# First x rows on ScalarE's queue, second rows' squares, scalings and transposes in blocks 3 to 7, rotary tables behind the context rows

## The chip, the cores and the metric

The kernel runs on one core of a Trainium2 chip. The core has TensorE (PE in the profile; its weight loads are PEld), VectorE (DVE), ScalarE (ACT), GpSimd (POOL) and SyncE (SP), each with an instruction queue of its own, and 16 DMA engines that all of them share. The metric is the device time of one execution in microseconds (us); the median of several runs is compared.

## The reference

One layer of a diffusion backbone over 1024 latent tokens and 256 context tokens, 1024 wide. What matters here is its very beginning: the modulation vectors, the normalised and modulated rows, and the first of seven blocks of columns of the input projection (the values of the differential attention, 512 columns).

```python
def rms_norm(x, g):
    xf = x.astype(jnp.float32)
    y = xf * lax.rsqrt(jnp.mean(xf * xf, axis=-1, keepdims=True) + EPS)
    return (y * g.astype(jnp.float32)).astype(x.dtype)
...
        m_lat = sc @ w_mod[l] + b_mod[l]
        m_ctx = scc @ w_mod[l] + b_mod[l]
        sh1, sc1, g1, sh2, sc2, g2 = [t[:, None, :] for t in jnp.split(m_lat, N_MOD, axis=-1)]
        csh1, csc1, cg1, csh2, csc2, cg2 = jnp.split(m_ctx, N_MOD, axis=-1)

        h_lat = rms_norm(x, norm1_g[l]) * (1.0 + sc1) + sh1
        h_ctx = rms_norm(ctx, norm1_g[l]) * (1.0 + csc1) + csh1
        y_lat, y_ctx = token_mixers(h_lat, h_ctx, w_in[l], ret_decay_logit[l], ret_gn_g[l],
                                    diff_lambda[l], diff_subln_g[l], w_out[l], lambda_init,
                                    rope_r, rope_d, need_ctx=not last)
```

Everything is in float32. The rest of the layer (retention, differential attention, output projection, gated MLP with a convolution, final norm) follows and is the larger part of the time; the change does not touch it.

## The kernel before, in words

A float32 product is made of three passes over split operands (`passes`, L126 to L131): high by high, high by low, low by high. So every operand exists as a pair, `hT[0]`/`hT[1]` for the rows (`cT` for the context) and `whi`/`wlo` for weights.

The first stage (L490 to L710) computes, for each of the eight blocks k of 128 input columns:

- **the modulation** of that block: two loads of w_mod of 512 KB each (`mod_load`, tile `wt`, five buffers), eight products (`mod_part`), a copy (`mod_row`, tile `rw`), four small products (`mod_sums`, tile `pm`) and two evictions into `mcol`;
- **the rows**, turned: `latents(half, k)` transposes the block's columns of four row tiles on TensorE (L545, into a PSUM tile `pt`), and `modulate` makes the high part on ScalarE (L548), the float32 value `tmp` on VectorE (L550) and the low part `hT <- tmp,hT` (L552) on VectorE for even k and on POOL for odd k. `half` 0 is tokens 0 to 511 (row tiles 0 to 3, `xs0`), `half` 1 is tokens 512 to 1023 (row tiles 4 to 7, `xs1`). `tmp` has two buffers; `pt`, `pm` and a few others share three PSUM banks;
- **the products** of row tiles 0 to 3 with block k of the weights (`part_products`), six matmuls for each pair of tiles.

Before its columns can be turned, a row tile is loaded, squared and summed on ScalarE (`square`, L533), brought to its reciprocal root by a small operation on VectorE and a power on POOL (`power`, L114 and L115), and scaled on VectorE (`scale`, L539). Column 2 to 5 of `sm` belong to row tiles 0 to 3, column 6 to 9 to row tiles 4 to 7, 0 and 1 to the two context tiles.

Row tiles 4 to 7 are multiplied after the loop over k, 24 matmuls each, from the weights that are then all split: tiles 4 and 5 in this stage, with the function `between` putting other work between their blocks (the last latents, the stores `st` of tiles 0 to 3, the squares and scales of the context rows `xc`, and from tile 5 on the context's transposes), tiles 6 and 7 behind it. At the start and between the first modulations, `turn_over` issues matmuls on a tile of ones whose result is not used.

Two things set the order. Inside the stage, `in_order(begin)` chains all instructions of PE, DVE, ACT and SP from L594 on in the order in which the code stands; POOL is left out. Outside it, a scheduler places instructions by their dependencies, and may put one of a later stage between two of this one, as it does with the first split of the next stage's weights (`stream_block(5)`, L183 to L187). Loads all go through SP's queue, in order; a load takes one of eight completion semaphores in turn, so that the ninth load waits until the first has landed, and so on.

Of the kernel before, what the change touches and what calls it, by code (L numbers as in the profile page):

```python
# [17 lines left out]
P = 128  # L18
D = 1024
KD = D // P  # L20
# [52 lines left out]
def kernel(  # L73
# [16 lines left out]
    nc = tc.nc  # L90
    mm = nc.tensor.matmul
# [34 lines left out]
    def passes(ps, lt, rt, first, last, more=False):  # L126
        lh, ll = lt
        rh, rl = rt
        mm(ps, lh, rh, start=first, stop=False, skip_group_check=more)  # L129
        mm(ps, lh, rl, start=False, stop=False, skip_group_check=more)  # L130
        mm(ps, ll, rh, start=False, stop=last, skip_group_check=more)  # L131
# [20 lines left out]
    with ExitStack() as p1:  # L152
# [20 lines left out]
        hT = [[hp.tile([P, KD, 512], F32R, name=f"hT{a}{i}") for i in range(2)] for a in range(2)]  # L173
        xs0 = [xr.tile([P, D], F32, name=f"xs{t}") for t in range(4)]
        cT = []
        sm = hp.tile([P, 16], F32, name="sm")
# [320 lines left out]
        with ExitStack() as p0:  # L497
# [77 lines left out]
            def load_row(t):  # L575
                nc.sync.dma_start(out=xs0[t] if t < 4 else xs1[t - 4], in_=x[t * P : (t + 1) * P, :])

# [5 lines left out]

            def part_products(ts, k):
                for t in ts:
                    passes(part[t], lat_lhs(t, k), wget(k, 0, 512), k == 0, k == KD - 1)

# [6 lines left out]
            mod_load(0, 0)  # L594
            for t in range(3):
                load_row(t)
            mod_load(0, 1)
            load_row(3)
            w_load(0, 2)
# [4 lines left out]
            mod_part(0, 0)  # L604
            turn_over(10)
            square(xs0[0], 2)
# [13 lines left out]
            mod_sums(0)  # L620
            turn_over(4)
            scale(xs0[2], 4)
# [11 lines left out]
            for k in range(KD):  # L634
# [4 lines left out]
                if k < 2:  # L639
                    for q in range(2):  # L640
                        mod_part(k + 2, q)
                    mod_row(k + 2)
                if k == 7:
                    latents(1, 2)
                    latents(1, 3)
                if 1 < k < 6:
                    load_row(k + 2)
                n = k + 4
# [15 lines left out]
                if k == 3:  # L664
                    square(xs1[0], 6)
                    power(6)
                if k == 4:
                    square(xs1[1], 7)
                    scale(xs1[0], 6)
                    power(7)  # L670
                if k == 5:
                    first.close()
                    cp = pctx.enter_context(tc.tile_pool(name="cp", bufs=1, side="right"))
                    cT.extend(cp.tile([P, KD, LC], F32R, name=f"cT{a}") for a in range(2))
                    for t in range(NTC):
                        xc.append(xp.tile([P, D], F32, name="xc", tag="wt", bufs=5))
                        nc.sync.dma_start(out=xc[t], in_=ctxt[t * P : (t + 1) * P, :])
                    square(xs1[2], 8)
                    scale(xs1[1], 7)
                    power(8)  # L680
                    square(xs1[3], 9)
                    scale(xs1[2], 8)
                    power(9)
                    scale(xs1[3], 9)
                if k >= 6:
                    latents(1, 4 * (k - 6))
                    latents(1, 4 * (k - 6) + 1)
            for t in range(2):
                store(t, part[t])

            def between(t, k):
                if (t, k) == (4, 0):
                    latents(1, 6)
                    latents(1, 7)
                if (t, k) == (4, 1):
# [31 lines left out]
        pad(m2p, 128)  # L727
        rtab = load_rope(1)
        natural(wget, lat_lhs, range(6, NT), store)
# [804 lines left out]
```

## Time and profile before

| | us |
|---|---|
| median of 3 runs | 1408.58 (1408.39 to 1412.42) |
| the profiled execution | 1407.91 |
| its span, first to last instruction | 1406.1 |
| PE busy in the span | 1366.5 (97%) |
| DVE, ACT, POOL busy | 991.4, 729.6, 287.5 |
| PE busy in 0 to 10, 10 to 20 us | 5.09, 8.00 |
| PE busy in 20 to 50 us | 30.0 |
| PE busy in 50 to 60, 60 to 70 us | 7.01, 8.37 |
| DMA in 10 to 20, 50 to 60 us | 418, 24 GB/s |

How to read the profile: times are from the start of the span of one execution. A group is written as line, engine, operation, then output <- inputs by the names of the tiles, partitions x elements. The chain of waits is followed back from the last instruction of the span, at each step to what released it. Matmuls overlap each other, so the distance of two starts says more than the length of one.

### The profile page before, as it was taken

Reading aid. Unit: us, or ns where it says so; the run is one execution under the profiler, and the core shown is the slowest. Engines: PE = TensorE matmul, PEld = TensorE weight load, DVE = VectorE, ACT = ScalarE, POOL = GpSimd, SP = SyncE. Lnnn points to the kernel's source line nnn. Section 1 sums busy time; section 2 is a strip of 40 time slices with the busy share of each in tenths; the row PEclk is TensorE's granted clock in tenths of the full one; section 3 lists DMA queues with packets and bytes.
Section 4 is the critical chain, followed back from the end, with each engine's and each line's share of the span. In section 5 each row is a group of like instructions: output and inputs, shape, how many; then the busy total and the mean of one; then the engine's idle time right before and its main releaser. Section 6 shows DMA issues by size and latency. Waiting matters only on the chain.

```text
span 1406.1 us, 19426 instructions
## 1 busy us (share of the span) xinstructions
PE 1366.5 (97%) x7028; PEld 1147.6 (82%) x7028; DVE 991.4 (71%) x1445; ACT 729.6 (52%) x1391; POOL 287.5 (20%) x321
## 2 busy tenths in 40 slices
PE   8899999999999899999999999999999999999996
PEld 5688888888887799998888778888888888888885
DVE  3655874424686798886458987777787777897457
ACT  3553313333575689997136645555445555455533
POOL 1310000001656033411201242233332220000001
PEclk9999999999999999999999999999999999999999
DMA  9546885465575597622321223323323226953224
GB/s 336 224 151 200 284 278 188 134 182 172 177 242 159 175 208 170 126 66 85 141 98 45 97 98 113 113 90 113 105 105 113 96 79 219 397 175 104 91 97 179
DMA packets 96807, 218.81 MB, mean 156 GB/s; under 512 B 9220, under 2 KB 31236, under 8 KB 96200
## 3 DMA queue, kind: packets, MB, share of 16 engines
q1 hardware_dynamic: 88552, 192.67, 40.0%
q0 software_dynamic: 8160, 24.91, 7.8%
q8 instruction: 55, 0.90, 0.3%
q14 instruction: 40, 0.33, 0.1%
HBM read 160.13 MB, written 57.41 MB: 155 GB/s over the span
## 4 chain that ended last, share of the span: by engine, by line
PE 81%; issue 5%; DMA 5%; DVE 4%; ACT 2%; POOL 2%; SPq 0%; POOLq 0%; ACTq 0%; DVEq 0%
PE pv L869 5%; PE chain L129 5%; PE pA L837 5%; PE chain L131 5%; PE chain L130 5%; PE c L131 4%; PE c L129 4%; PE c L130 4%; PE pn L129 4%; PE pn L131 4%; PE pn L130 3%; PE pl L129 3%; PE pl L131 3%; PE pl L130 3%; PE third L129 2%
## 5 line engine op out<-in xcount | busy, mean ns | idle before, releaser
L129 PE MATMUL chain<-T,whi 128*128 128x512 f32 x264 | 103.5, 393 | 4.9 <-ACT ua L1250 3.9
L129 PE MATMUL pl<-hT,whi 128*128 128x512 f32 x256 | 106.2, 415 | 0.0
L130 PE MATMUL chain<-T,whi 128*128 128x512 f32 x264 | 103.5, 392 | 0.0
L131 PE MATMUL chain<-T,wlo 128*128 128x512 f32 x264 | 103.3, 392 | 0.0
L131 PE MATMUL pl<-hT,wlo 128*128 128x512 f32 x256 | 100.2, 391 | 0.0
L130 PE MATMUL pl<-hT,whi 128*128 128x512 f32 x256 | 100.0, 391 | 0.0
L840 DVE TENSOR_REDUCE mt<-pA 128x1 f32<-128x1280 f32 x64 | 95.3, 1490 | 3.6 <-PE pA L837 2.8
L837 PE MATMUL pA<-ks,qhl 128*128 128x512 f32 (+1 forms) x384 | 89.5, 369 | 2.7 <-ACT p L844 2.7
L131 PE MATMUL c<-whi,ghl 128*128 128x512 f32 x232 | 90.4, 390 | 0.0
L130 PE MATMUL c<-wlo,ghl 128*128 128x512 f32 x232 | 90.3, 389 | 0.0
L129 PE MATMUL c<-whi,ghl 128*128 128x512 f32 x232 | 90.3, 389 | 0.0
L844 ACT ACTIVATE p<-pA,mt 128x1280 f32<-128x1280 f32 x64 | 85.5, 1336 | 6.7 <-DVE mt L840 6.7
L1008 ACT CAST whi<-cmb 128x512 fp32r<-128x512 f32 x62 | 38.6, 623 | 86.7 <-PE chain L130 65.3
L837 PEld LDWEIGHTS pA<-ks,qhl 128*128 128x128 f32 x384 | 67.6, 189 | 14.8 <-ACT p L844 3.4
L129 PE MATMUL pn<-whi,hT 128*128 128x512 f32 x192 | 79.1, 412 | 0.0
L1163 POOL TENSOR_TENSOR cmb<-wrb 128x512 f32<-128x512 f32 x20 | 27.2, 1360 | 248.7 <-DMA wrb<-w_up 165.6
L869 PE MATMUL pv<-va,aT 128*128 128x128 f32 x640 | 77.0, 275 | 0.1
L131 PE MATMUL pn<-whi,hT 128*128 128x512 f32 x192 | 75.6, 394 | 0.9 <-POOL hT L552 0.4
L130 PE MATMUL pn<-wlo,hT 128*128 128x512 f32 x192 | 75.6, 394 | 0.0
L869 PEld LDWEIGHTS pv<-va,aT 128*128 128x128 f32 x640 | 74.0, 192 | 0.7 <-DVE yT L898 0.3
L1009 DVE TENSOR_TENSOR wlo<-cmb,whi 128x512 fp32r<-128x512 f32 x62 | 57.0, 922 | 23.0 <-ACT whi L1008 23.0
L115 POOL TENSOR_TENSOR sm<-sm,mhalf 128x1 f32<-128x1 f32 x26 | 17.0, 657 | 274.0 <-DVE sm L114 273.9
(300 smaller groups left out, 3812.7 us busy)
## 6 DMA issues: line engine op xcount, KB each, us to landing
wm<-w_mod SPq DMA_DIRECT2D x32, 512.0 KB, 5.1
raw<-w_in SPq DMA_DIRECT2D x27, 512.0 KB, 4.6
wra<-w_up SPq DMA_DIRECT2D x24, 512.0 KB, 3.4
wrb<-w_up SPq DMA_DIRECT2D x23, 512.0 KB, 3.5
W<-w_down SPq DMA_DIRECT2D x44, 256.0 KB, 6.2
ad<-s SPq DMA_DIRECT2D x20, 512.0 KB, 3.6
wra<-ad SPq DMA_DIRECT2D x20, 512.0 KB, 3.3
kvs<-kvg SPq DMA_DIRECT2D x36, 256.0 KB, 3.2
```

What stands on the lines that cost most here:

```text
L115: nc.gpsimd.tensor_tensor(out=out_ap, in0=out_ap, in1=mhalf[:, :n], op=ALU.pow)
L129: mm(ps, lh, rh, start=first, stop=False, skip_group_check=more)
L130: mm(ps, lh, rl, start=False, stop=False, skip_group_check=more)
L131: mm(ps, ll, rh, start=False, stop=last, skip_group_check=more)
L837: mm(self.pa[m][:, c0:c1], self.q[:, m, i, qs], self.k[:, m, c0:c1], start=(i == 0), stop=(i == 1))
L840: nc.vector.tensor_reduce(out=self.mt[:, m : m + 1], in_=self.pa[m][:, :LK], axis=AX.X, op=ALU.min)
L844: nc.scalar.activation(self.p[m], self.pa[m][:, :LK], AF.Exp, scale=-1.0, bias=self.mt[:, m : m + 1], accum_out=self.s[:, m : m + 1])
L869: mm(self.pv, self.aT[:, c, :], self.v[:, c, :], start=(c == 0), stop=(c == NKT - 1))
L1008: nc.scalar.copy(hi, src)
L1009: nc.vector.tensor_tensor(out=lo, in0=src, in1=r32(hi), op=ALU.subtract)
L1163: nc.gpsimd.tensor_tensor(out=s1, in0=b1, in1=b2, op=ALU.add)
```

## The change

Four things.

1. The loads of row tiles 0 to 3 move from SP's queue, where they stood between the first two loads of w_mod, to the head of ScalarE's queue. `load_row` is left for row tiles 4 to 7, each issued one block earlier. Six `turn_over` matmuls in front of the second modulation load go, four come in front of the first transposes.
2. At k = 0 the passes of two tiles are done as hi, lo, hi, lo and then both low ones, in place of three by three.
3. Squares and powers of row tiles 4 and 5 stand in block 3 and those of 6 and 7 in block 4, the scales of 4 and 5 in block 4 and those of 6 and 7 between the two halves of block 5; `latents(1, 0)` to `latents(1, 7)` stand two by two behind the two halves of blocks 6 and 7, so that none is left in tile 4.
4. The rotary tables are loaded inside the ordered stretch, behind the context rows. Before, the scheduler had put these two loads ahead of the context rows.

```diff
@@ -172,6 +172,8 @@
         xs0 = [xr.tile([P, D], F32, name=f"xs{t}") for t in range(4)]
+        for t in range(4):
+            nc.scalar.dma_start(out=xs0[t], in_=x[t * P : (t + 1) * P, :])
         cT = []
@@ -573,7 +575,7 @@
             def load_row(t):
-                nc.sync.dma_start(out=xs0[t] if t < 4 else xs1[t - 4], in_=x[t * P : (t + 1) * P, :])
+                nc.sync.dma_start(out=xs1[t - 4], in_=x[t * P : (t + 1) * P, :])
@@ -582,8 +584,16 @@
             def part_products(ts, k):
+                if k > 0:
+                    for t in ts:
+                        passes(part[t], lat_lhs(t, k), wget(k, 0, 512), False, k == KD - 1)
+                    return
+                hi, lo = wget(k, 0, 512)
                 for t in ts:
-                    passes(part[t], lat_lhs(t, k), wget(k, 0, 512), k == 0, k == KD - 1)
+                    mm(part[t], lat_lhs(t, k)[0], hi, start=True, stop=False)
+                    mm(part[t], lat_lhs(t, k)[0], lo, start=False, stop=False)
+                for t in ts:
+                    mm(part[t], lat_lhs(t, k)[1], hi, start=False, stop=False)
@@ -592,17 +602,14 @@
             mod_load(0, 0)
-            for t in range(3):
-                load_row(t)
             mod_load(0, 1)
-            load_row(3)
             w_load(0, 2)
...
             mod_part(0, 0)
-            turn_over(10)
+            turn_over(4)
             square(xs0[0], 2)
@@ -618,7 +625,7 @@
             mod_sums(0)
-            turn_over(4)
+            turn_over(8)
             scale(xs0[2], 4)
@@ -640,11 +647,14 @@
-                if k == 7:
-                    latents(1, 2)
-                    latents(1, 3)
-                if 1 < k < 6:
-                    load_row(k + 2)
+                if k == 5:
+                    scale(xs1[2], 8)
+                    scale(xs1[3], 9)
+                if k >= 6:
+                    latents(1, 4 * (k - 6))
+                    latents(1, 4 * (k - 6) + 1)
+                if 0 < k < 5:
+                    load_row(k + 3)
@@ -663,11 +673,16 @@
                 if k == 3:
                     square(xs1[0], 6)
+                    square(xs1[1], 7)
                     power(6)
+                    power(7)
                 if k == 4:
-                    square(xs1[1], 7)
                     scale(xs1[0], 6)
-                    power(7)
+                    scale(xs1[1], 7)
+                    square(xs1[2], 8)
+                    square(xs1[3], 9)
+                    power(8)
+                    power(9)
@@ -675,23 +690,14 @@
-                    square(xs1[2], 8)
-                    scale(xs1[1], 7)
-                    power(8)
-                    square(xs1[3], 9)
-                    scale(xs1[2], 8)
-                    power(9)
-                    scale(xs1[3], 9)
                 if k >= 6:
-                    latents(1, 4 * (k - 6))
-                    latents(1, 4 * (k - 6) + 1)
+                    latents(1, 4 * (k - 6) + 2)
+                    latents(1, 4 * (k - 6) + 3)
+            rtab = load_rope(1)
             for t in range(2):
                 store(t, part[t])
 
             def between(t, k):
-                if (t, k) == (4, 0):
-                    latents(1, 6)
-                    latents(1, 7)
                 if (t, k) == (4, 1):
@@ -725,7 +731,6 @@
         pad(m2p, 128)
-        rtab = load_rope(1)
         natural(wget, lat_lhs, range(6, NT), store)
```

**Place one: the head of the queues.** SP before, from its first load on (`wt` is w_mod, `raw` the weights, `xs_172` to `xs_175` the row tiles 0 to 3):

```order
L98 DMA cl<-cols 128x260
L107 DMA ident<-consts 128x128
L511 DMA wt<-w_mod 128x1024
L576 DMA xs_172<-x 128x1024
L576 DMA xs_173<-x 128x1024
L576 DMA xs_174<-x 128x1024
L511 DMA wt<-w_mod 128x1024
L576 DMA xs_175<-x 128x1024
L565 DMA raw<-w_in 128x512 x2
```

ScalarE in the changed program, with the semaphores waited for (`DMAHW0` to `DMAHW7` are the eight of the loads):

```order
L176 DMA xs_172<-x 128x1024
L176 DMA xs_173<-x 128x1024
L176 DMA xs_174<-x 128x1024
L176 DMA xs_175<-x 128x1024 [waits DMAHW0_49]
L181 ACT_TABLE_LOAD
L181 ACTIVATE csil<-cl 128x16 [waits DMAHW1_49]
L535 ACTIVATE sq,sm<-xs_172 128x1024
L535 ACTIVATE sq,sm<-xs_173 128x1024 [waits DMAHW4_49,Activation_49]
```

The four loads left SP for the head of ScalarE; semaphore 0 is that of the first of them, so the fourth is issued when the first has landed, and ScalarE's own first instructions stand behind it.

**Place two: VectorE from block 4 to the second half's latents.** Before (`xs_0` to `xs_3` are row tiles 4 to 7, `mcol` the evictions of block 7's modulation):

```order
L573 TENSOR_TENSOR wlo<-raw,whi 128x1024
L539 TENSOR_SCALAR xs_0_203<-xs_0_203,sm 128x1024
L114 TENSOR_SCALAR sm<-sm 128x1
L528 TENSOR_SCALAR mcol<-pm,bsc,cl 128x2
L529 TENSOR_SCALAR mcol<-pm,cl 128x2
L550 TENSOR_SCALAR tmp<-pt,mcol 128x512
L539 TENSOR_SCALAR xs_1_204<-xs_1_204,sm 128x1024
L114 TENSOR_SCALAR sm<-sm 128x1
L539 TENSOR_SCALAR xs_2_205<-xs_2_205,sm 128x1024
L114 TENSOR_SCALAR sm<-sm 128x1
L539 TENSOR_SCALAR xs_3_206<-xs_3_206,sm 128x1024
L550 TENSOR_SCALAR tmp<-pt,mcol 128x512
```

Changed, from the same split on:

```order
L575 TENSOR_TENSOR wlo<-raw,whi 128x1024
L541 TENSOR_SCALAR xs_0_207<-xs_0_207,sm 128x1024
L541 TENSOR_SCALAR xs_1_208<-xs_1_208,sm 128x1024
L114 TENSOR_SCALAR sm<-sm 128x1 x2
L541 TENSOR_SCALAR xs_2_209<-xs_2_209,sm 128x1024
L541 TENSOR_SCALAR xs_3_210<-xs_3_210,sm 128x1024
L530 TENSOR_SCALAR mcol<-pm,bsc,cl 128x2
L531 TENSOR_SCALAR mcol<-pm,cl 128x2
L189 TENSOR_TENSOR wlo<-raw,whi 128x1024
L552 TENSOR_SCALAR tmp<-pt,mcol 128x512 x2
```

All four scales now stand ahead of block 7's `mcol`, and the scheduler has put the next stage's first split (L189) between that and block 7's `tmp`; before, it stood behind the fifth `tmp` of the second half.

**Place three: ScalarE from the squares of row tiles 6 and 7 to those of the context.** Before:

```order
L533 ACTIVATE sq,sm<-xs_2_205 128x1024
L533 ACTIVATE sq,sm<-xs_3_206 128x1024
L548 ACTIVATE hT_169<-pt,mcol 128x512 x4
L186 COPY whi<-raw 128x1024
L548 ACTIVATE hT_169<-pt,mcol 128x512 x2
L394 ACTIVATE st<-pn 128x512 x2
L548 ACTIVATE hT_169<-pt,mcol 128x512 x2
L394 ACTIVATE st<-pn 128x512 x2
L533 ACTIVATE sq,sm<-xc 128x1024 x2
```

Changed:

```order
L535 ACTIVATE sq,sm<-xs_2_209 128x1024
L535 ACTIVATE sq,sm<-xs_3_210 128x1024
L188 COPY whi<-raw 128x1024
L550 ACTIVATE hT_168<-pt,mcol 128x512
L550 ACTIVATE hT_169<-pt,mcol 128x512 x8
L396 ACTIVATE st<-pn 128x512 x4
L535 ACTIVATE sq,sm<-xc 128x1024 x2
```

The first two `st`, which stood ahead of the last two `hT` of the second half, stand behind all eight of them now, directly ahead of the other two and of the squares of the context rows.

## Prediction

> **What bounds the kernel now.** I read the page first, then stages of 10 us, then the chain of waits and the timelines where TensorE is not busy.
>
> ```profile
> span 1406.1 us, 19426 instructions
> PE 1366.5 (97%) x7028; PEld 1147.6 (82%) x7028; DVE 991.4 (71%) x1445; ACT 729.6 (52%) x1391; POOL 287.5 (20%) x321
> ```
>
> TensorE is 97% busy, so what the change can win is TensorE's idle time in its own stretch, the first 75 us. The stages (window, length, busy us and instructions of PE, PEld, DVE, ACT, POOL, then granted clock, DMA share, GB/s):
>
> ```profile
> 0.00:10.00 10.00, 5.09 (x25) 4.02 (x26) 1.30 (x11) 2.84 (x5) 0.59 (x6) 1.00 0.78 251
> 10.00:20.00 10.00, 8.00 (x63) 5.40 (x62) 6.27 (x14) 5.81 (x11) 3.06 (x4) 1.00 1.03 418
> ...
> 50.00:60.00 10.00, 7.01 (x32) 5.61 (x31) 4.86 (x10) 4.06 (x8) 4.06 (x4) 0.83 0.06 24
> 60.00:70.00 10.00, 8.37 (x45) 6.49 (x44) 8.30 (x12) 8.37 (x14) 5.21 (x4) 1.00 0.44 157
> 70.00:80.00 10.00, 10.00 (x53) 8.15 (x52) 7.21 (x14) 5.18 (x10) 3.39 (x6) 1.00 0.07 28
> ```
>
> There are two holes: the start, and 50 to 70, where 4.6 us are idle and the granted clock falls to 0.83 as well. Between them and from 70 on TensorE has no gap for long. So two places are costed, and what is won by 72 stays won, since TensorE's instructions behind it stand in one order in both programs.
>
> **The start.** The chain of waits there (start, us, what), and the first product from the timeline:
>
> ```profile
> 4.40 9.08 DMA xs<-x
> 13.56 1.15 ACT sq L533 x2
> ...
> 18.29 0.70 DVE hT L552
> ...
> 19.54 0.23 PE pn L129
> ```
> ```profile
> 17.88 0.50 PE L129 MATMUL pn<-whi,hT 128*128 128x512 f32 x1
> ```
>
> The fourth x row is issued at 4.40 and lands at 13.48; square, power, scale, transpose and `hT` bring the first product 4.4 us later, at 17.88. The third pass then waits for the low half, subtracted from 18.29 to 19.0. The new order of passes at k = 0 puts two matmuls of the second tile into that wait; at the 0.23 us from one 512-column matmul to the next this wins **0.46 us**.
>
> The x rows themselves go to ScalarE's queue. There the fourth waits for the first one's landing, and the table load and `csil` stand behind it:
>
> ```profile
> 0.74 1.28 ACT L179 ACT_TABLE_LOAD   x1 [0.74 <-PEq L1527]
> 2.96 0.22 ACT L179 ACTIVATE csil<-cl 128x16 f32<-128x16 f32 x1 [0.94 <-DMA cl<-cols]
> 8.51 1.06 ACT L533 ACTIVATE sq<-xs 128x1024 bf16<-128x1024 f32 x1 [5.33 <-DMA xs<-x]
> 12.94 0.37 ACT L521 COPY rw<-pr 128x256 f32<-128x256 f32 x1 [0.76 <-PE pr L517]
> ```
>
> If the first row lands 1 us sooner, at 7.5, issue (0.5, as on SP), table load and `csil` put the first square near 9.5. Four squares of 1.15 (chain) to 1.25 and the `rw` copy before the last make that end at 14.8 at the earliest, which costs nothing if the fourth row lands later than 13.6. When does it? No load of this trace is on ScalarE's queue, but one pair of rows shows what two queues do: the same 512 KB store of SP, issued once at 447.71 with little beside it and once at 453.80 beside POOL's loads (issue rows, then the two queues over 450 to 470).
>
> ```profile
> dq<-xhl SPq DMA_DIRECT2D x1, 512.0 KB, 3.4
> ...
> dq<-xhl SPq DMA_DIRECT2D x1, 512.0 KB, 13.2
> ...
> q0 software_dynamic: 1616, 4.06, 79.3%
> q1 hardware_dynamic: 1206, 1.78, 28.4%
> ```
>
> 13.2 us in place of 3.4: a queue of its own does not go ahead, it shares. Now the bytes. By 13.48 the engines had moved 10 us x 251 GB/s + 3.48 us x 418 GB/s = 3.96 MB; queued up to the fourth row were `cl` and `ident`, 0.2, and six loads of 0.524, together 3.34 MB. A load lands 0.6 MB behind its place. Shared evenly, the four rows (2.10 MB) are through when SP's queue has moved as much; SP can issue 2.29 MB by then without waiting for anything large. 4.2 + 0.6 = 4.8 MB is 0.84 MB, or 2.0 us, later than now. Against that, bytes flow sooner:
>
> ```profile
> 2.13 1.51 SPq L576 DMA_DIRECT2D xs<-x  x3
> ```
>
> ScalarE can issue its first row at 0.74, where its table load starts now, 1.39 us before SP does; I credit 1.0 of it, since the first 10 us already run at 251 GB/s, not at 418. So the fourth row lands **1.0 us later**, at 14.5.
>
> Bounds: if the x rows go first, the first one skips a w_mod load (0.524 MB, 1.25 us) and lands at 8.5 - 1.25 - 1.0 = 6.3, the squares end at 13.6 instead of 14.7, a gain of 1.1. If SP's queue goes first, with 2.29 MB and two more loads, the rows need 5.4 + 0.6 = 6.0 MB, 5.0 us later less 1.0, a loss of 4.0. I take the even share, because here the packets of both queues are rows of 4 KB, while the store's packets (1.78 MB / 1206 = 1.5 KB) stood against 2.5 KB of POOL's.
>
> The Trainium skill ("DMA: Bandwidth & Descriptors", section "Queues, rings and completion order") says that each DMA engine takes turns between queues with work, packet by packet; the 13.2 us agree. Its section "Rules for kernel authors" adds that loads spread over several issuing engines win no bandwidth, which speaks against this part of the change; by that the start is lost as in my sum.
>
> The start: 1.0 - 0.46 = **+0.5 us**, between -1.6 and +3.5. The moved `turn_over` matmuls fill waits of TensorE and are costed at nothing; the four more in front of the first transposes have 128 columns each, so they take less than 4 x 0.23 us, hidden as long as the fourth row is waited for.
>
> **Blocks 5 to 7 and tile 4.** What makes the hole, from the timeline:
>
> ```profile
> 35.09 0.93 SPq L576 DMA_DIRECT2D xs<-x  x2
> 45.98 1.06 ACT L533 ACTIVATE sq<-xs 128x1024 bf16<-128x1024 f32 x1
> 48.17 0.47 PE L129 MATMUL pn<-whi,hT 128*128 128x512 f32 x1
> 50.32 1.06 ACT L533 ACTIVATE sq<-xs 128x1024 bf16<-128x1024 f32 x1
> 53.32 0.56 POOL L115 TENSOR_TENSOR sm<-sm,mhalf 128x1 f32<-128x1 f32 x1 [0.93 <-DVE sm L114]
> 53.91 0.75 DVE L539 TENSOR_SCALAR xs<-xs,sm 128x1024 f32<-128x1024 f32 x1 [0.67 <-POOL sm L115]
> 56.27 0.63 PE L130 MATMUL pn<-wlo,hT 128*128 128x512 f32 x1
> ...
> 69.94 0.39 PE L129 MATMUL pn<-whi,hT 128*128 128x512 f32 x1
> ```
> ```profile
> DMA to landing us min/median/max: 7.1/8.0/9.1
> ```
>
> The last line is of the view on the x tiles. The eighth x row is squared at 50.32 and scaled at 53.91, so the transposes that need it run at 54.7, and the matmuls behind them run at a lower clock (rows of 0.63 us where others have 0.39). In the new order I keep the clock of the old trace (the start's term is added at the end).
>
> ScalarE: the seventh row's square takes the place at 45.98, the eighth's follows at 47.15 and ends at 48.3. The eighth row is issued in the place of 35.09, no later than now; with 8.0 us from issue to landing it is there at 43, 4 us in time, and the three before it are issued a block earlier. VectorE: `wlo` to 47.3, scales 6 and 7 to 48.7, POOL's two powers of 0.55 to 49.95, scales 8 and 9 to 50.9. TensorE has done block 6's first six matmuls at 48.17 + 6 x 0.23 = 49.6 and waits 1.0 us for that last scale, not 3.9.
>
> After that VectorE is the pace. Behind scale 9 stand the two `mcol` (0.5), the next stage's `wlo` (1.22) and the `tmp` of latents 7, which ends at 53.3 and frees a PSUM bank of three. Then four pairs:
>
> ```profile
> 61.93 1.22 DVE L187 TENSOR_TENSOR wlo<-raw,whi 128x1024 fp32r<-128x1024 f32 x1
> 62.09 2.18 POOL L552 TENSOR_TENSOR hT<-tmp,hT 128x512 fp32r<-128x512 f32 x1 [2.42 <-DVE tmp L550]
> 63.06 0.81 DVE L550 TENSOR_SCALAR tmp<-pt,mcol 128x512 f32<-128x512 f32 x1
> 63.90 0.92 DVE L552 TENSOR_TENSOR hT<-tmp,hT 128x512 fp32r<-128x512 f32 x1
> ...
> 68.27 1.28 POOL L552 TENSOR_TENSOR hT<-tmp,hT 128x512 fp32r<-128x512 f32 x1 [1.35 <-DVE sm L114]
> ```
>
> Two `tmp` of 0.8 and one subtraction of 0.70 (chain) to 0.92 make 2.45 us a pair, so the last `tmp` ends at 53.3 + 9.8 = 63.1 and POOL's last subtraction (1.3) at 64.4. TensorE gets its banks at 53.3, 54.0, 55.7, 56.4, 58.1 and 58.9; its last transposes end at 59.4, tile 4's 24 matmuls (5.5 us) at 65.0, with the last low half at 64.4 just in time. Tile 5 starts at 65.1 instead of 69.94: 4.8 us won.
>
> **Then a new wait.** Tile 5 needs the context rows, and what is late next is their square:
>
> ```profile
> 63.18 0.81 SPq L400 DMA_DIRECT2D dvd<-st  x2
> 66.13 0.60 ACT L394 ACTIVATE st<-pn 128x512 f32<-128x512 f32 x1 [0.24 <-DMA dvd<-st]
> 66.62 1.05 ACT L533 ACTIVATE sq<-xc 128x1024 bf16<-128x1024 f32 x1
> 70.09 1.58 DVE L539 TENSOR_SCALAR xc<-xc,sm 128x1024 f32<-128x1024 f32 x2 [0.96 <-POOL sm L115]
> 71.72 0.55 PE L545 MATMUL pt<-ident,xc 128*128 128x128 f32 x3
> ```
>
> On ScalarE all four `st` now stand behind all eight `hT` of the second half. The last `hT` ends at 60.3, the first two `st` at 61.4. The next two need those buffers back, 2.5 us after their stores' issue (the fourth `st` at 66.13 waited for the store of about 63.6), so they end at 64.3. The squares run 64.3 to 66.6, power and two scales (0.2 + 0.55, then two at 0.75) to 68.3, and the context transposes run at 68.3 instead of 71.72: **3.4 us won**, the other 1.4 of 4.8 lost to this wait.
>
> Bounds: 4.8 if the wait is hidden; 1.7 if pairs take 3.0 us, as where VectorE's and POOL's passes overlap (POOL's subtraction took 2.18 at 62.09, 1.28 at 68.27): the last low half then comes near 67, its powers 1.1 later, the context scales at 69.9.
>
> The rope tables behind the context rows land in a stretch that moves 24 GB/s and are first used in the next stage; without that cover two loads would cost 2.5 us.
>
> **Sum:** +0.5 - 3.4 = -2.9 us. The profiled execution took 1407.91 (span 1406.1 and 1.8 around it), so 1405.0; the median of the runs shown lies 0.67 higher, so I say **1405.7**.
>
> **Rivals.**
> 1. The start is not lost: the x rows go first, or the sooner bytes pay for the sharing. The 251 GB/s of the first stage speaks for it (two queues may fill it better), the 13.2 us against. Start -1.6, then -3.4: -5.0, 1403.6; with the new wait hidden too, 1402.2.
> 2. The pairs take 3.0 us: +0.5 - 1.7 = -1.2, 1407.4.
> 3. Nothing is won in blocks 5 to 7, because the eighth row lands over 4 us later than reckoned and ScalarE stands at its square with all `hT` behind it. Against it: SP issues it no later than now. +0.5, 1409.1.
> 4. Slower: SP's queue goes first and the fourth row lands 4.0 us later. TensorE then idles over 3 us before the first product and starts at the lower clock, as after the hole before 54.7; the stage's granted 0.83 over 10 us prices that at 1.7. +3.5 + 1.7 - 3.4 = +1.8, 1410.4. It decides from a landing of the fourth row after 17.3, or 15.6 with the clock lost.
>
> **How the numbers follow.** Forecast 0.45, rivals 0.33, 0.11, 0.04, 0.07. The range of the bounds is -6.4 to +1.8, 1402.2 to 1410.4; I cut the top, where little chance lies: 1402.0 to 1409.8. A measurement of this kernel tells 0.3%, 4.2 us, from no change. Faster than 1404.35: rival 1 and a little of the forecast's edge less rival 1's own, 0.33. Slower than 1412.8: part of rival 4, 0.04. Within: 0.63.
>
> **What would show it.** First square near 9.5; the fourth row's square near 14.6, first product near 18.9, two passes and two more before the low ones. No half clock between 50 and 60; transposes of the second half between the products of blocks 6 and 7 with a wait of about 1 us for scale 9. TensorE waiting some 1.5 us for `xc` in tile 5. I am wrong about the queues if the fourth square starts before 13.5, about the pairs if tile 4 ends after 66.5, and about the new wait if tile 5 shows none.

## The result, and the profile after

| | before | changed kernel |
|---|---|---|
| median of 20 runs each, us | 1408.57 (1406.79 to 1412.80) | 1406.24 (1401.14 to 1410.38) |
| profiled execution, us (span) | 1407.91 (1406.1) | 1407.36 (1405.2) |
| first product of block 0 / block 1, us | 17.88 / 24.25 | 19.19 / 25.44 |
| first product of tile 5, us | 69.94 | 66.74 |
| first product of the next stage (`pl`), us | 99.15 | 95.89 |

The ratio of the times is 0.9974, 95% interval 0.9965 to 0.9983: 2.4 to 4.9 us faster. The means are 1405.87 and 1409.42, 3.5 apart; the medians are 2.3 apart. The middle of the interval, 0.26%, is under the 0.3% that the prediction took as what can be told from no change, though the interval leaves out 1, which would be no change; 1405.7 was predicted. The last row of the table is the landmark used below. It lies behind all that the change touches, so its shift is what the change itself did: 3.26 us sooner in this execution. From TensorE's timeline, of before and then of the changed kernel (start, us, instruction):

```profile
99.15 0.39 PE L129 MATMUL pl<-hT,whi 128*128 128x512 f32 x1
```
```profile
95.89 0.39 PE L129 MATMUL pl<-hT,whi 128*128 128x512 f32 x1
```

The page of the changed kernel, and its stages of 10 us (columns as in the prediction):

```profile
span 1405.2 us, 19416 instructions
PE 1367.5 (97%) x7024; PEld 1147.1 (82%) x7024; DVE 994.1 (71%) x1445; ACT 729.3 (52%) x1391; POOL 285.3 (20%) x321
```
```profile
0.00:10.00 10.00, 2.31 (x12) 2.01 (x16) 2.22 (x13) 3.69 (x6) 1.72 (x7) 1.00 0.79 272
10.00:20.00 10.00, 9.60 (x72) 6.71 (x64) 3.77 (x10) 4.53 (x9) 2.31 (x3) 1.00 1.03 416
...
50.00:60.00 10.00, 9.25 (x49) 6.44 (x48) 9.24 (x13) 5.51 (x8) 4.10 (x5) 1.00 0.81 307
60.00:70.00 10.00, 9.91 (x48) 7.74 (x46) 6.59 (x10) 6.35 (x11) 5.25 (x5) 1.00 0.34 130
```

The hole from 50 to 70 is closed (9.25 and 9.91 busy for 7.01 and 8.37, granted clock 1.00 for 0.83). The start is worse: 2.31 us busy in the first stage for 5.09. The second stage's 9.60 for 8.00 is no gain: w_mod's first product has slid into it, and matmuls take longer there, as the chain of waits of the first 20 us shows (start, us, what):

```profile
1.66 7.97 DMA wt<-w_mod
9.63 0.14 issue
9.77 1.08 PE pr L519 x8
10.85 2.01 PE pn L600 x8
12.86 1.01 PE pr L519 x8
...
16.33 0.16 DVE sm L114
...
17.52 0.36 DVE xs L541
...
18.30 0.79 ACT hT L550
```

In the kernel before, this chain ran over the fourth x row. Now it begins with w_mod's first load, which lands at 9.63 (its product started at 6.98 before). `turn_over` (L600) lies on it too, at 0.25 us a matmul. ScalarE's rows from the timeline give the other end of the chain:

```profile
6.78 1.04 ACT L535 ACTIVATE sq<-xs 128x1024 bf16<-128x1024 f32 x1
13.94 0.37 ACT L523 COPY rw<-pr 128x256 f32<-128x256 f32 x1 [2.62 <-PE pr L519]
14.20 1.06 ACT L535 ACTIVATE sq<-xs 128x1024 bf16<-128x1024 f32 x1
```

The first row's square comes 1.7 sooner than before. The fourth row's square follows the copy `rw` at once, with no DMA named in front of it: it waits for TensorE, not for its row.

Bytes over the first 5.5 us (stages 0 to 5.5, last column GB/s), before and then the changed kernel:

```profile
0.00:5.50 5.50, 2.07 (x8) 1.78 (x8) 1.15 (x10) 1.50 (x2) 0.52 (x5) 1.00 0.58 131
```
```profile
0.00:5.50 5.50, 2.08 (x8) 1.78 (x8) 0.57 (x6) 0.14 (x1) 0.52 (x5) 1.00 0.67 209
```

That is 5.5 x 131 = 0.72 MB and 5.5 x 209 = 1.15 MB: more is moved while the loads begin. A part of it is earlier issue, since the first row is now issued at 0.74, for 2.13 before.

Blocks 6 and 7 and tiles 4 and 5 in the changed kernel's timelines (the DVE rows at 55.20 and 56.28 are VectorE's part of one pair of `latents`):

```profile
50.53 1.58 DVE L541 TENSOR_SCALAR xs<-xs,sm 128x1024 f32<-128x1024 f32 x2 [0.60 <-POOL sm L115]
52.16 0.98 PE L547 MATMUL pt<-ident,xs 128*128 128x128 f32 x5 [0.50 <-DVE xs L541]
54.51 1.38 PE L547 MATMUL pt<-ident,xs 128*128 128x128 f32 x8
55.20 1.16 DVE L554 TENSOR_TENSOR hT<-tmp,hT 128x512 fp32r<-128x512 f32 x1
56.28 1.52 DVE L552 TENSOR_SCALAR tmp<-pt,mcol 128x512 f32<-128x512 f32 x2
57.13 1.38 PE L547 MATMUL pt<-ident,xs 128*128 128x128 f32 x8
59.76 1.37 PE L547 MATMUL pt<-ident,xs 128*128 128x128 f32 x8
64.56 1.22 ACT L396 ACTIVATE st<-pn 128x512 f32<-128x512 f32 x2 [1.62 <-DMA dvd<-st]
66.74 0.39 PE L129 MATMUL pn<-whi,hT 128*128 128x512 f32 x1
69.34 0.75 DVE L541 TENSOR_SCALAR xc<-xc,sm 128x1024 f32<-128x1024 f32 x1 [0.45 <-POOL sm L115]
```

The view of waits names one wait of TensorE from 40 to 75, the 0.50 for the eighth row's scale. The pairs run 2.62 and 2.63 apart, and VectorE sets that: its two `tmp` take 1.52 and its subtraction 1.16. TensorE's own work allows less, since a pair took 2.27 before (transposes at 58.30 and 60.57); its eight transposes now stretch over 1.38, for 1.04 then. The store copy waits 1.62 for its buffer, so the context rows are ready only at 69.34 + 0.75 = 70.1, 3.4 us behind tile 5's start; yet TensorE doesn't wait for them. The order of its instructions tells why. Its last product ahead of the first context transpose, and that transpose, before and then in the changed kernel:

```profile
71.10 0.39 PE L131 MATMUL pn<-whi,hT 128*128 128x512 f32 x1
71.33 0.27 PE L545 MATMUL pt<-ident,xc 128*128 128x128 f32 x1
```
```profile
69.72 0.39 PE L130 MATMUL pn<-wlo,hT 128*128 128x512 f32 x1
69.95 0.27 PE L547 MATMUL pt<-ident,xc 128*128 128x128 f32 x1
```

Tile 5 starts at 69.94 before and at 66.74 now, and its products follow each other at 0.23 us: 14 of them stand ahead of the first context transpose, where the kernel before had 6. The change's own lines don't say so. Eight more products of 0.23 are 1.8 us of cover.

What was won by 96 us stands to 780. Then the profiled execution loses 1.5 between 785 and 1179, where it has a lower clock at waits that the kernel before has as well (stage 790 to 800, before and then the changed kernel, granted clock in the third column from the end), and 0.85 at one wait for VectorE behind 1206:

```profile
790.00:800.00 10.00, 7.13 (x31) 5.28 (x30) 7.41 (x7) 6.63 (x9) 8.81 (x6) 1.00 0.59 222
```
```profile
790.00:800.00 10.00, 7.45 (x24) 5.67 (x25) 8.75 (x10) 7.75 (x11) 6.68 (x4) 0.83 0.30 110
```

The lower clock there is not the change's doing: e4, e8 and e9 below run the same instructions there, and the stage reads 1.00 in e4 and e8 and 0.83 in e9. So the two spans differ by 0.9 only, while the medians differ by 2.3 and the means by 3.5.

### The profile page after: what moved, and what is told of

It is laid out like the page before. It is cut to its first block, busy times and chain, and to the rows that moved or that the text cites. A ratio compares the mean times of both kernels' runs of the same rounds, so it can differ in the third digit from the quotient of the medians.

```text
span 1405.2 us, 19416 instructions
## 1 busy us (share of the span) xinstructions
PE 1367.5 (97%) x7024; PEld 1147.1 (82%) x7024; DVE 994.1 (71%) x1445; ACT 729.3 (52%) x1391; POOL 285.3 (20%) x321
## 4 chain that ended last, share of the span: by engine, by line
PE 78%; DMA 6%; issue 5%; DVE 5%; POOL 2%; ACT 2%; SPq 0%; POOLq 0%; ACTq 0%; DVEq 0%
PE pv L874 5%; PE chain L129 5%; PE chain L130 5%; PE chain L131 5%; PE pA L842 5%; PE c L131 4%; PE c L129 4%; PE c L130 4%; PE pn L129 3%; PE pn L131 3%; PE pn L130 3%; PE pl L129 2%; PE pl L131 2%; PE pl L130 2%; PE third L129 2%
## 5 line engine op out<-in xcount | busy, mean ns | idle before, releaser
L129 PE MATMUL pn<-whi,hT 128*128 128x512 f32 x188 | 76.7, 408 | 0.0
L131 PE MATMUL pn<-whi,hT 128*128 128x512 f32 x188 | 73.6, 392 | 0.0
```

## Experiments

For each kernel: the first product, the start of block 1 (its first product), the first product of the next stage (all from TensorE's timelines), and the time against the kernel before on the same chip. The experiments ran on three chips, so that the ratios, not the medians, compare from row to row.

| kernel | first product | block 1 | next stage | median, us | ratio, 95% interval |
|---|---|---|---|---|---|
| before | 17.88 | 24.25 | 99.15 | | |
| changed | 19.19 | 25.44 | 95.89 | 1406.24 | 0.9974 (0.9965 to 0.9983) |
| e1_queue_alone | 21.09 | 27.80 | 102.75 | 1412.93 | 1.0023 (1.0014 to 1.0033) |
| e2_rows_on_sync | 19.98 | 26.23 | 96.54 | 1408.79 | 0.9993 (0.9983 to 1.0003) |
| e3_square_first | 19.47 | 25.75 | 96.24 | 1406.50 | 0.9981 (0.9972 to 0.9990) |
| e4_three_by_three | 19.42 | 26.14 | 96.63 | 1405.65, one run | |
| e5_rows_and_turns_back | 18.04 | 23.98 | 94.23 | 1404.51 | 0.9963 (0.9951 to 0.9975) |
| e6_turns_late | 17.13 | 23.38 | 93.86 | 1407.86 | 0.9987 (0.9976 to 0.9998) |
| e7_wmod_on_scalar | 16.39 | 22.67 | 92.94 | 1405.40 | 0.9972 (0.9961 to 0.9983) |
| e8_context_early | 18.51 | 24.76 | 95.49 | 1406.44 | 0.9976 (0.9965 to 0.9988) |
| e9_rope_back | 19.03 | 25.28 | 95.75 | 1406.36, one run | |
| e10_scales_alone | 17.89 | 23.77 | 96.19 | 1405.49 | 0.9979 (0.9969 to 0.9989) |
| e11_transposes_alone | 17.84 | 24.12 | 99.30 | 1409.36 | 1.0006 (0.9993 to 1.0018) |
| e12_power_first | 16.33 | 22.32 | 92.60 | 1404.16 | 0.9975 (0.9962 to 0.9987) |

All but the times comes from one execution of each kernel, and such numbers scatter. The changed kernel, e8 and e9 have the same start, and their block 1 comes at 25.44, 24.76 and 25.28; e5, e10 and e11 share another, with block 1 at 23.98, 23.77 and 24.12. A difference of up to 0.7 at the start can be chance. The distance from block 1 to the next stage scatters less (70.45 and 70.47 in the changed kernel and e9).

**The rows' queue alone, on the kernel before.**

```diff
+        for t in range(4):
+            nc.scalar.dma_start(out=xs0[t], in_=x[t * P : (t + 1) * P, :])
...
             mod_load(0, 0)
-            for t in range(3):
-                load_row(t)
             mod_load(0, 1)
-            load_row(3)
```

> The kernel before with one edit: its four first x rows on ScalarE's queue. Theory A (the rows share the DMA engines with w_mod's first load, which then lands near 9.6; ScalarE's copy of its product stands ahead of the fourth square, so the row has landed and waits): no DMA wait in front of the fourth square, it starts near 14.2, first hT near 18.3 (before 16.64), first product near 19.2, block 1 near 26.1 (before 24.49); the whole at most 1.7 us slower, 1408.6 to 1410.3. Rival B (as predicted: the fourth row itself lands 1.0 later): a DMA wait in front of the fourth square near 14.5, first product near 18.9. Rival C (nothing lost at the start): first product at 17.9 or sooner, 1408.6.

Theory A holds in kind, but the price is over twice its own (3.2 for 1.3 at the first product), and the whole loses 3.3 by the ratio where A allowed 1.7. The timelines of e1:

```profile
10.58 4.64 PE L592 MATMUL pn<-ones 128*128 128x128 f32 x20
15.14 0.96 PE L519 MATMUL pr<-wt,cz 128*32 128x256 f32 x8
...
16.18 0.37 ACT L523 COPY rw<-pr 128x256 f32<-128x256 f32 x1 [5.23 <-PE pr L519]
16.45 1.06 ACT L535 ACTIVATE sq<-xs 128x1024 bf16<-128x1024 f32 x1
```

The fourth square starts without a DMA wait, behind `rw`, as A has it. But the ten `turn_over` of the old count (20 matmul records, two to each) now begin at 10.58, behind w_mod's late first product at 9.57, and last to 15.2. Before, they ran from 7.99 to 11.6, ahead of w_mod's second load, which TensorE then still waited for. So w_mod's second product, and with it `rw`, now waits for these matmuls. That the twenty take 4.64 here and took 3.62 before is no effect of the queue: with the rows on SyncE they take 3.56 in e10 and 4.54 in e11. So the rows' queue without the new counts costs 3.2 at the first product and 0.23% of the whole.

**The rows back on SyncE, all else as changed.**

```diff
-        for t in range(4):
-            nc.scalar.dma_start(out=xs0[t], in_=x[t * P : (t + 1) * P, :])
...
             mod_load(0, 0)
+            for t in range(3):
+                load_row(t)
             mod_load(0, 1)
+            load_row(3)
```

> The changed kernel with its four first x rows back on SyncE's queue in the old order. Theory A (the rows' queue costs the start 1.66 at the first hT, and all else of the change stays won): first hT near 16.6, first product near 17.9, block 1 near 24.0, tile 5 near 65.1 (changed kernel 66.74), the first product of the stage behind the natural tiles near 94.2 (changed 95.9, before 99.2); 1406.24 - 1.7 = 1404.5, ratio to before 0.997. Rival (the later start is made up for in blocks 5 to 7, where VectorE is the pace): tile 5 near 66.7 and 95.9, 1406.2.

A miss for both theories: the fourth square is back at 13.78, but the first `hT` comes at 19.09, later than in either kernel, and the whole loses most of its gain. TensorE's timeline of e2:

```profile
12.37 1.08 PE L517 MATMUL pr<-wt,cz 128*32 128x256 f32 x8 [2.19 <-DMA wt<-w_mod]
...
15.11 3.51 PE L598 MATMUL pn<-ones 128*128 128x128 f32 x16
18.45 0.60 PE L545 MATMUL pt<-ident,xs 128*128 128x128 f32 x4
```

With four `turn_over` in place of ten TensorE waits 2.19 for w_mod's second load; its product then takes 1.08 instead of 0.64, and the eight `turn_over` behind the row sums take 3.51 (0.22 a matmul). Both hold up the first `hT`: against e5 below, the fourth row's scale, behind the late row sums on VectorE, comes 1.4 later (17.46 for 16.04), and from there to the first `hT` it takes 0.9 longer, while the eight `turn_over` end. The counts are a part of the change with a price of its own, and they don't fit the old queue.

**Rows and counts back.** e2 with `turn_over(10)` and `turn_over(4)` in place of 4 and 8.

> The kernel of e2_rows_on_sync with the turn_over matmuls too at their old counts, 10 behind w_mod's first product and 4 behind the row sums. Theory T (the ten keep TensorE at speed through the wait for w_mod's second load; in e2 it fell to half speed there, and its eight turn_overs took 3.5 us in front of the first transposes): the second product takes 0.64 again instead of 1.08, the turn_overs behind the row sums some 1.1, first hT near 16.6 and first product near 17.9 (e2: 19.09, 19.98), the first product of the stage behind the natural tiles near 94.5 (changed 95.9, e2 96.5); 1404 to 1405, ratio 0.997. Rival (another part of the change delays the start): first hT near 19, 96.5, as e2.

Theory T holds: the second product takes 0.64 at 12.40, first `hT` at 16.81, first product at 18.04, next stage at 94.23. The ten bring TensorE to speed rather than keep it there, since in e2 the eight records ahead of the wait took 2.08, 0.26 each. Without the rows' queue and its counts, the change wins 4.92 at the next stage instead of 3.26, and 0.37% of the whole; that interval and the changed kernel's overlap.

**When does the fourth row land?**

```diff
             turn_over(2)
+            square(xs0[3], 5)
             mod_row(0)
             power(4)
             scale(xs0[1], 3)
-            square(xs0[3], 5)
+            scale(xs0[2], 4)
+            power(5)
+            turn_over(8)
             mod_sums(0)
-            turn_over(8)
-            scale(xs0[2], 4)
-            power(5)
+            scale(xs0[3], 5, 0, 2 * P)
             w_split(0, 1)
-            scale(xs0[3], 5, 0, 2 * P)
```

> The changed kernel, rows still on ScalarE's queue, with the fourth square ahead of the row copy on ScalarE, and third scale and fourth power ahead of the row sums on VectorE; the eight turn_over matmuls ahead of the row sums on TensorE. Theory A (the fourth row has landed long before 14.2 and only stands behind the copy): the fourth square starts between 11.3 and 13, first hT near 16.1 (mcol at 15.6 then gates it), first product near 17.0, 2.2 sooner than in the changed kernel; the stage behind the natural tiles near 93.7; 1404.0. Rival B (the row lands near 14.2 anyway): a DMA wait in front of the fourth square, first hT near 17.3, first product near 18.2, 1405.2.

The timeline of e3 answers the question, and shows what takes the gain:

```profile
12.38 1.06 ACT L535 ACTIVATE sq<-xs 128x1024 bf16<-128x1024 f32 x1 [1.24 <-DMA xs<-x]
...
13.62 3.48 PE L600 MATMUL pn<-ones 128*128 128x128 f32 x20
```

The row lands at 12.38, 1.1 sooner than the 13.48 of before, not 1.0 later. Theory A is right on the row and wrong on the gain (first product 19.47 for its 17.0). Nothing was won by it, since ten `turn_over` (2 + 8) now stood ahead of the row sums and took 3.48.

**The same with the `turn_over` matmuls out of the way.** On the changed kernel: none between w_mod's first two products, four behind the second, two behind the row sums; third scale and fourth power ahead of the row sums as in e3, but `rw` ahead of the fourth square.

> The changed kernel, rows on ScalarE's queue; no turn_overs between w_mod's first two products, four behind the second (2 there now), two behind the row sums (8 now), the fourth square still behind the row copy, third scale and fourth power ahead of the row sums. Theory T (the fourth row lands at 12.35, as in e3; only the cold turn_overs ahead of w_mod's second product, and through it the row copy, hold its square at 14.2): second product at 10.9, row copy near 12.0, fourth square near 12.4, fourth row's scale near 14.7, first hT near 15.5, first product near 16.5 (changed 19.19, before 17.88); first product of the next stage near 93.2; 1403.5. Rival (w_mod's second load lands late): second product still near 12.7 with a DMA wait, first product near 18.

```profile
11.47 1.08 PE L519 MATMUL pr<-wt,cz 128*32 128x256 f32 x8 [1.34 <-DMA wt<-w_mod]
...
12.89 1.06 ACT L535 ACTIVATE sq<-xs 128x1024 bf16<-128x1024 f32 x1
```

w_mod's second load lands at 11.4, between the two expectations; in the changed kernel its product starts at 12.79, so 1.3 of the delay there are `turn_over`. The first product comes at 17.13, 2.1 sooner than in the changed kernel and 0.75 sooner than before, with the rows on ScalarE's queue all the same. The next stage starts 5.3 sooner than before, but the whole is only 0.13% faster (1.8), where some 5 were expected.

**The queues exchanged.** w_mod's first two loads on ScalarE's queue, the four rows on SyncE's, `rw` behind the second square, `csil` behind the loads' issue, six `turn_over` ahead of the row sums and six behind:

```diff
+            mod0 = [xp.tile([P, 4, 2 * P], F32, name="wt", bufs=5) for _ in range(2)]
+            for q in range(2):
+                nc.scalar.dma_start(out=mod0[q], in_=w_mod[0][:, 4 * q : 4 * q + 4, :])
...
-            mod_load(0, 0)
-            mod_load(0, 1)
+            for t in range(4):
+                load_row(t)
```

> The changed kernel with the queues exchanged: w_mod's first two loads on ScalarE's queue, the four x rows on SyncE's; turn_overs six behind w_mod's second product and six behind the row sums, the row copy behind the second square. Theory Q (two queues move 0.43 MB more in the first 5.5 us, and w_mod's loads no longer stand behind or beside all rows): w_mod's first product near 6.5, fourth square near 12.4, first product near 16.4; next stage near 93.1; 1403.4. Rival (no bandwidth won): fourth square near 13.5, first product near 17.5.

Theory Q holds at the start: w_mod's two products run at 6.96, the fourth square at 11.67 directly behind the third's, the first product at 16.39, 1.5 sooner than before. That is not the queues' alone, since `rw` and the counts moved too, and moves of that kind won 0.75 in e6. The next stage starts 6.2 sooner than before, but the median is only 4.3 lower (3.9 by the ratio). An addition to it (`power(5)` ahead of `scale(xs0[2], 4)`):

> The kernel of e7_wmod_on_scalar with the fourth row's power ahead of the third row's scale on VectorE and POOL's side (in e7 that power waited behind a scale that itself waited for POOL). Theory (the chain of the fourth row ends 0.7 sooner, and what is won at the start is kept up to the next stage): first product near 15.7 (e7 16.39), next stage near 92.3 (e7 92.9); the whole 6 us sooner than before less what later drops of the granted clock take, 1403 to 1405. Rival (in blocks 5 to 7 something that doesn't depend on the start takes over, the landing of a row): next stage at 92.9 as in e7.

First product at 16.33 instead of 15.7, next stage at 92.60: 6.55 won there, and 4.4 by the medians (3.5 by the ratio). Against e7 that is 0.06 and 0.34 sooner, no more than the scatter of such traces, so neither theory is shown.

**The order of the passes.** Block 0's passes three by three again.

> The changed kernel with the passes of block 0 back in the old order, three of one tile and then three of the other. Theory (two 512-column matmuls fill the wait for the low half): block 1 starts 0.46 later than in the changed kernel, near 26.15, and the stage behind the natural tiles near 96.4 (95.9). Rival (the wait for the low half is ended by VectorE all the same, and block 1 waits for its own operands): block 1 near 25.7, 95.9.

The first product is 0.23 later than in the changed kernel, block 1 0.70: the order of the passes is worth 0.47.

**The wait for the context rows.**

```diff
                 if (t, k) == (4, 1):
+                    for i in range(2):
+                        square(xc[i], i)
+                        power(i)
                     for i in (2, 3):
                         store(i, part[i])
-                if t == 4 and k in (3, 5):
-                    i = (k - 3) // 2
-                    square(xc[i], i)
-                    power(i)
```

> The changed kernel with the two squares and powers of the context rows in front of the third and fourth store copy on ScalarE, so that they no longer wait for the store buffers. The build then places the first context transposes behind tile 5's sixth matmul, as in the kernel before; in the changed kernel they stand behind its fourteenth. Theory O (in the changed kernel the wait costs nothing, since eight matmuls of 0.23 stand ahead of the transposes): context transposes some 1.8 sooner, near 68.2, and the first product of the next stage at 95.9 as now, 1406.2. Rival (as predicted: the wait for the context rows costs 1.4): next stage near 94.5, 1404.8.

Theory O holds. The context transposes come at 67.45, 2.5 sooner (block 1 is 0.68 sooner), but from block 1 to the next stage nothing is won: 70.73 instead of 70.45.

**The second half: which of the two moves wins?** On e5, first with the transposes of the second half back at their old places, then with its squares, powers and scales back.

> The kernel of e5_rows_and_turns_back (start as before, first product near 18.0, next stage at 94.2 against 99.15 before) with the second half's transposes back at their old places; its squares and scales stay in blocks 3 to 5. Theory S (the hole from 50 to 58 is the wait for the eighth row's scale; the moved scales win, the transposes' place decides little): no stage of 10 us under granted 0.9 between 50 and 60, next stage near 95.0, most of the 4.9 kept. Rival P (the transposes' place wins): next stage near 98.

> The kernel of e5_rows_and_turns_back with the second half's squares, powers and scales back at their old places in blocks 3 to 5; its transposes stay in the middle and at the end of blocks 6 and 7, and the loads of the rows stay one block earlier. Theory S: the transposes in the middle of block 6 wait for the eighth row's scale near 54, with block 6's last six matmuls behind them; next stage at 98.5 to 100, nothing won but the 0.46 of the passes. Rival P (the transposes' place wins, or the earlier loads do): next stage near 95.

TensorE's stage of 50 to 60 in e10 and in e11, and its waits in e11 from 40 to 78 (us in total, times, longest):

```profile
50.00:60.00 10.00, 8.32 (x41) 6.67 (x40) 7.41 (x11) 4.11 (x6) 2.84 (x3) 0.83 0.65 256
```
```profile
50.00:60.00 10.00, 6.08 (x22) 4.91 (x23) 4.62 (x9) 3.37 (x7) 4.03 (x4) 0.66 0.69 265
```
```profile
PE pt L545 <- DVE sm L114: 3.1, 2, 2.1
PE pt L545 <- DVE xs L539: 1.0, 1, 1.0
```

From block 1 to the next stage it takes 74.90 before, 70.25 in e5, 72.42 in e10 and 75.18 in e11. So the early scales win 2.5 by themselves, and the granted clock still falls once, which S had excluded; e10's next stage, 96.19, lies between S's 95.0 and P's 98. The moved transposes add 2.2 behind early scales; alone (e11) they lose 0.3, since block 6's last products then stand behind the wait for the scales. S is right that the scales come first, but once they are early the transposes' place is worth nearly as much.

**The rotary tables back behind the padding.**

> The changed kernel with the two loads of the rotary tables back behind the padding, where they stood before. Theory (they land in a stretch with free DMA engines and are used much later): the first product of the stage behind the natural tiles within 0.5 of the changed kernel's 95.9, no TensorE wait for the tables. Rival (two loads of cover are missed): a wait of up to 2.5 in the stage that uses them, 98.4.

As the theory has it: from block 1 to the next stage 70.47 against 70.45.

## Why the prediction was right, and where it was not

The time (1406.24 for 1405.7) and the sum came out: -2.9 predicted, -3.26 at the next stage. Three terms of the sum were off, and they cancelled; that the sum is so close is luck.

**The start: +0.5 predicted, +1.19 at block 1 (1.66 at the first `hT` less 0.47 of the passes).** In e9 and e8, with the same start, it is +1.0 and +0.5, so how far the size was off stays open. The way to it was wrong. The step that failed is "the fourth row lands 1.0 us later". It lands 1.1 sooner (e3). Three things were wrong in it. The first row: it lands near 4.9, 4.2 us after its issue, where 7.5 was assumed, so that the fourth is issued sooner and the first square starts at 6.78, not 9.5. The bytes: 0.43 MB more moved in the first 5.5 us, where the prediction set 1.0 us of earlier issue against 2.0 of sharing. And the load that the rows delay: w_mod's first, from 6.95 to 9.63 (to 9.57 by the queue's edit alone, e1). The prediction followed the rows alone, because they were the chain of the kernel before, and left out what that load feeds: two products and `rw`, which stands ahead of the fourth square on ScalarE. The sign I had set, a fourth square before 13.5, couldn't show the mistake, since the square waited for `rw`. The rest of the 1.66 (fourth square 0.64 later) is on VectorE: the row sums, late now, stand ahead of the third row's scale and of the fourth's L114, which runs 2.13 behind its square's start, for 1.43 before; the power and scale behind it take 0.3 longer.

The Trainium skill ("DMA: Bandwidth & Descriptors", section "Rules for kernel authors") has it that spreading loads over issuing engines doesn't help bandwidth and saves only issue time. In the first 5.5 us more did move here, 209 GB/s for 131, but the first row was also issued 1.39 us sooner, and no run separates the two; from 5.5 to 10 us this case agrees, with 350 GB/s for 397.

**"The moved `turn_over` matmuls are costed at nothing."** That failed too. With the rows back on SyncE, the new counts cost 2.25 at block 1 (e2 against e5); with the rows on ScalarE, the old counts bring 27.80 (e1) for e4's 26.14. The sizes were wrong as well: the working put one `turn_over` under 0.23 us because it has 128 columns, but at 13.83 in the kernel before four of them take 1.14, 0.28 each. From idle their matmuls take twice as long (0.25 us a record for 0.13), and in the changed kernel those from idle hold w_mod's second product up by 1.3 (e6). The Trainium skill ("TensorE: Matmul & The Clock Gate", Part 1) says that the array starts at half clock and is released by some 3.4 us of sustained work; the two speeds agree, with 0.25 us for one `turn_over` matmul from idle and 0.13 for those behind the row sums. The time is longer in some executions here: in e1 TensorE works from 9.57 on, and w_mod's second product at 15.14 still takes 0.96 where 0.64 is its time at speed.

**The passes:** 0.46 predicted, 0.47 measured (e4).

**Blocks 5 to 7 and tile 4: 4.8 won, predicted; 4.39 measured** (tile 5 3.20 sooner, from a block 1 that was 1.19 later). The mechanism was right: a wait of 0.5 for scale 9 (1.0 predicted), no stage at 0.83, VectorE as the pace. The term mis-sized is the pair, 2.62 instead of 2.45: three steps make the 0.5. VectorE's subtraction takes 1.16 while POOL's runs beside it, where the working had 0.70 to 0.92. Taking off the 1.19 of the start, tile 4 ends at 65.55, under the 66.5 that would have made rival 2 right. e10 and e11 show the working's part on the squares and scales at work, and that the transposes' new place carries 2.2 of it, which the prediction hadn't split.

**"Then a new wait": 1.4 predicted, 0 measured.** The wait on ScalarE is there (1.62 for the store buffer), and the context rows are ready at 70.09, 68.9 without the 1.19 of the start, for 68.3 predicted. The step that failed is "Tile 5 needs the context rows": needed they are behind its fourteenth product, not its sixth, in the order as built. I took the place from the kernel before. e8 shows it: the rows ready sooner and the transposes back behind the sixth product win nothing. This is the half of rival 1 that came true; its other half, a start not lost, didn't.

**The rotary tables:** nothing, as costed (e9).

**From 96 us to the end.** -3.26 became -0.9 in the profiled execution, -2.3 in the medians and -3.5 in the means, so over all runs no loss is shown. Of the changed kernel's 20 runs, those with a mean granted clock of 0.997 took 1401.1 to 1404.3, those with 0.995 took 1405.3 to 1410.4. Of the start experiments, e5's 4.9 are whole at the end (0.37%, 5.2); of e7's 6.2 arrive 3.9, of e12's 6.55 3.5, and of e6's 5.3 only 1.8 (by the ratios). Profiles show where in two of them, those with the queues exchanged: e7 loses 3.5 between 357 and 461, with TensorE waiting 3.5 for the `qk` loads between 340 and 400, for 1.5 in the changed kernel, and a granted clock of 0.95 and 0.88 in the two stages from 360 to 380. e12 waits 3.5 there too, at 0.89 and 0.94; all other traces read 1.00 in these two stages.

Why an earlier arrival should lose there stays open: no run tells it. So e5, e7 and e12 are faster than before, and which is the best of them, or by how much they beat the changed kernel, the intervals don't say.

## What to carry to other kernels

When a load is moved to a second queue, follow the loads it now shares with, not itself: the one that lost was the first w_mod load, and it held the moved row's work through one copy on ScalarE. Filler matmuls belong to the waits they were counted for; move the waits and they turn from cover into work ahead of the chain. And where a tile's place in the built order decides whether a wait costs anything, read that place in the changed program, not in the old one.

## What was not expected of the hardware

- The granted clock of the stages reads 1.00 from 0 to 20 us in the changed kernel, while one `turn_over` matmul takes 0.25 us at 10.85 and those behind the row sums 0.13 (2.03 for 16): at the start the column doesn't show how fast TensorE runs; the durations do.
- The same 20 `turn_over` records behind w_mod's first product, with the rows on SyncE, took 3.62 before, 4.22 in e5, 3.56 in e10 and 4.54 in e11: when TensorE comes to speed differs from execution to execution.
- With the rows on a second queue 209 GB/s moved over the first 5.5 us where 131 had, and w_mod's first load landed 2.7 us later.
- Two waits in one place, of 1.01 and 1.86 us, ran on at a granted 1.00 in one profiled execution (stage 790 to 800 before), and in another, of 0.86 and 1.85, at 0.83 (the changed kernel). e8 and e9, the same instructions there, read 1.00 and 0.83.
